# A Fourier and Hyena encoder layer on one core: the filter network's two hidden layers with the positions' halves stacked on the partitions

## The chip, the cores and the metric

The kernel runs on one core of a Trainium2 chip. The metric is the device time of one execution in microseconds, as the median of several runs. Its engines are TensorE (PE in the profile, PEld for its weight loads), VectorE (DVE), ScalarE (ACT), GpSimd (POOL) and SyncE (SP, which issues most DMAs).

## The reference

The layer is applied to two inputs of 1024 positions by 1024 channels. Each goes through an RMS norm and one projection; a Fourier branch takes a two-dimensional DFT (over positions and over 256 channels of each of four groups) of one part; a Hyena branch runs two long convolutions whose filters come from a small network over the positions; both are gated, projected, merged and added to the input. The change touches the filter network, which does not depend on the inputs:

```python
pos = jnp.arange(L, dtype=f32)                       # L = 1024
t = pos / (L - 1)
bands = jnp.linspace(1e-4, FILT_BANDS - 1, FILT_BANDS, dtype=f32)
ang = (2.0 * math.pi * pos / L)[:, None] * bands[None]
z = jnp.concatenate([t[:, None], jnp.cos(ang), -jnp.sin(ang)], axis=-1)   # 1024 x 33
h = jnp.sin(f1 * (z @ w1 + b1))                      # 1024 x 64
h = jnp.sin(f2 * (h @ w2 + b2))                      # 1024 x 64
h = (h @ w3).reshape(L, N_DIR, H_ORDER, H_WIDTH)
h = h * jnp.exp(-t[:, None, None, None] * jnp.abs(decay)[None])
h = h / jnp.sum(jnp.abs(h), axis=(0, 1), keepdims=True)
# ... the two directions form one kernel of length 2L per channel, and its rfft
```

## The kernel before, in words

Nearly all matmuls take operands split into a rounded part and a remainder (`split`: ScalarE rounds, `sub` on VectorE or GpSimd makes the remainder) and run as three products (`mm3`, L193).

The program has a Fourier phase (to about 220 us), a main phase that begins with the filter stage (16 rounds, one for each order and channel tile, to about 480 us; projections are put between as filling work) and goes on with the convolutions, then gates and outputs.

**Fourier phase.** For the first input, `norm` loads eight row tiles `x`, squares each on ScalarE (`sq`, L319), and after each four of them computes `rs` on VectorE (`rstd`, L241 to L252) and four diagonal tiles `dg` (L324). `xtile` transposes and scales with matmuls against `dg` (`tpx`), writes `xg` on ScalarE (L343), stores it (`d_x`), and forms sums and differences `eo` and their split `eh`, `el`. `weights` loads one block of the projection's weights (`wfv`, two buffers, SP queue), forms `wer`, `wor` and splits them (`we`, `wo`). The projection matmuls `pfv` take both. Behind the first input's norm the table `seq` (2 MB) is loaded on GpSimd's queue. There are four Fourier halves, in the order (input 0, half 0), (0, 1), (1, 1), (1, 0); `fourier_half` runs pfv, the alternating column's `pfx` with its cast `x5t`, the sequence stage (`pse`, `pso`, `sev`, `sst`) and the channel stage (`pP`, `pQ`). The last forms `fA` and `fB` on VectorE, one buffer each, which GpSimd's queue stores to `d_fz`.

**Hidden layers.** `hidden(0, ...)` is called ahead of the first norm, `hidden(1, ...)` behind the third Fourier half. Each runs a plain f32 matmul `phd` (L296) for each half of the 1024 positions and `sin_of` (L258 to L270): seven VectorE steps of argument reduction on 128x512 and one sine on ScalarE. The weights stand twice side by side (33x128, 64x128), so that all 128 output partitions hold the 64 channels twice; the result `hd` is 128x1024 and goes to DRAM (`d_h1`, `d_h`). Layer 2 loads 64 of its rows.

**Rounding of hid.** `phase_main` loads `d_h` into `hidr`, rounds all of it to `hid` on ScalarE (L884) and puts the remainder in partitions 64 to 127, so one matmul with doubled weights `w3s` takes both (`pft`). In program order this stands behind the whole Fourier phase.

**Order.** The order within each engine is not the program's: a planner with its own cost model re-orders the instructions under their dependencies and buffers (`schedule_with_timeline_sim=True`). `tc.issue_after(i)` tells it to place what follows behind instruction `i`.

Of the kernel before, what the change touches and what calls it, by code (L numbers as in the profile page):

```python
# [9 lines left out]
F32 = mybir.dt.float32  # L10
F32R = mybir.dt.float32r
I32 = mybir.dt.int32
AF = mybir.ActivationFunctionType
# [3 lines left out]
P = 128  # L17
D = 1024
L = 1024
# [27 lines left out]
def _tables():  # L47
    t = {}
    s = np.arange(P) + 0.5
    fwd, in0, inv = [], [], []  # L50
    th = np.zeros((P, 8, 6))
    for pi, (f1, hf) in enumerate(PAIRS):
        f = f1 + 8 * (np.arange(P) + P * hf)
        w = 2 * np.pi * f / 2048
        c, sn = np.cos(np.outer(s, w)), np.sin(np.outer(s, w))
        wt = np.full(P, 1 / 1024.0)
        if f1 == 0:
            sn[:, 0] = np.sin(np.pi * s)
# [36 lines left out]
    t["c_alt"] = ae.astype(np.float32).reshape(P, 2 * 86)  # L95
    c = np.arange(P)
    cg = np.cos(2 * np.pi * np.outer(c, c) / 256) / 512
    sg = np.sin(2 * np.pi * np.outer(c, c) / 256) / 512
    sg[0] = 0.0
    sg[:, 0] = 0.0  # L100
    d0 = np.zeros((P, P))
    d0[:, 0] = (1.0 - 2.0 * (c % 2)) / 512
    t["c_chan"] = _hl(np.concatenate([cg, sg, d0], axis=1))
    xs = np.zeros((P, 2, 2, P))
    for g in range(2):
        for r in (g, 32 + g):
# [12 lines left out]
    for m in range(4):  # L119
        order.append(256 * m + 128 + np.arange(P))  # L120
        order.append(256 * m + 127 - np.arange(P))
    order = np.concatenate(order)
    t["c_z"] = np.ascontiguousarray(z[order].T)
    v = np.zeros((P, 14), f32)
    v[:, 0:8] = -tn[order].reshape(8, P).T
    v[:, 8] = 1.0
    v[127, 8] = 0.0
    v[127, 9] = 1.0
    v[1:, 10] = -1.0
    v[1:, 11] = 1.0  # L130
    v[:, 12] = -1.0
    v[0, 12] = 1.0
    t["c_vec"] = v
    t["c_id"] = np.eye(P, dtype=f32)
    return t
# [25 lines left out]
class K:  # L161
# [11 lines left out]
        self.left = self.sub(eng, l, src, h)  # L173

    def stt(self, eng, out, a, s, b, op0=MUL, op1=ADD):
        self.nc.vector.scalar_tensor_tensor(out, a, s, b, op0=op0, op1=op1)  # L176

    def tt(self, eng, out, a, b, op):
        e = self.nc.gpsimd if eng == "pool" else self.nc.vector
# [16 lines left out]
    def setup(self, ctx):  # L196
        tc, nc, a = self.tc, self.nc, self.a
# [18 lines left out]

        def dt(name, shape, dtype=F32):
            return dr.tile(shape, dtype, name=name)
        self.d_h = dt("d_h", [P, L])
        self.d_h1 = dt("d_h1", [P, L])  # L220
        self.d_x = [[dt(f"d_x{b}_{k}", [P, L]) for k in range(8)] for b in range(NB)]
        self.d_fz = [[dt(f"d_fz{b}_{k}", [P, L]) for k in range(8)] for b in range(NB)]
        self.d_k = [[dt(f"d_k{n}_{c}", [P, 32 * P]) for c in range(8)] for n in range(2)]
# [47 lines left out]

    def hidden(self, layer, px, pf):

        nc, a = self.nc, self.a
        h = px.tile([P, L], F32, tag="eo", name=f"hd_{layer}", bufs=2)
        out = [h[:, 0:512], h[:, 512:1024]]
        z = px.tile([P, L], F32, tag="x", name="hd_z", bufs=3)
        if layer == 0:
            w = pf.tile([P, P], F32, tag="sst", name="hd_w", bufs=1)
            self.hfb = px.tile([P, 4], F32, name="hd_fb", bufs=1)  # L280
            nc.sync.dma_start(z[0:33], a["c_z"])
            nc.scalar.dma_start(w[0:33], a["filt_w1"])
            nc.scalar.dma_start(self.hfb, a["filt_fb"])
            w, z = w[0:33], z[0:33]
            y, k = [[pf.tile([P, 512], F32, tag=f"{t}p{n}", name=f"s{t}", bufs=1 + (t == "p")) for n in range(2)]
                    for t in "qp"]
        else:
            nc.sync.dma_start(z[64:128], self.d_h1[64:128])
            w = px.tile([P, P], F32, tag="xg", name="hd_w", bufs=2)
            nc.sync.dma_start(w[64:128], a["filt_w2"])  # L290
            w, z = w[64:128], z[64:128]
            y, k = [px.tile([P, L], F32, tag="x", name="s" + t, bufs=3) for t in "yk"]
            y, k = [[t[:, 0:512], t[:, 512:1024]] for t in (y, k)]
        for n in range(2):
            p = self.psum("mm", 4, "phd")
            nc.tensor.matmul(p, w, z[:, 512 * n:512 * n + 512], start=True, stop=True)  # L296
            self.sin_of(y[n], k[n], out[n], p, self.hfb[:, 2 * layer:2 * layer + 1],
                        self.hfb[:, 2 * layer + 1:2 * layer + 2])
        nc.sync.dma_start(self.d_h if layer else self.d_h1, h)


# [80 lines left out]
    def fourier_half(self, b, half, W, fo, px, pf, begun={}):  # L382

        nc = self.nc
# [58 lines left out]
        vec = self.vec  # L443
# [6 lines left out]
        for g in range(2):  # L450
# [3 lines left out]
            A = pf.tile([P, 1026], F32, tag="fA", name="fA", bufs=1)  # L454
            B = pf.tile([P, 1026], F32, tag="fB", name="fB", bufs=1)
            gg = 2 * half + g
            for n in range(2):
                w = (258, 256)[n]
                ns = slice(258 * n, 258 * n + w)
                pr, qr = (Pp[0][:, ns], Pp[1][:, ns]), (Qp[0][:, ns], Qp[1][:, ns])  # L460
                pP = self.psum("X", 2, "pP")[:, :w]
                self.mm3(pP, (ch[:, 0, 0:P], ch[:, 1, 0:P]), pr, True, False)
                self.mm(pP, cx[:, 0, g, :], PX[:, ns], False, True)
                pQ = self.psum("X", 2, "pQ")[:, :w]
# [4 lines left out]
                Ps = pf.tile([P, 258], F32, tag="fPs", name="fPs", bufs=2)  # L469
                Pm = pf.tile([P, 258], F32, tag="fPm", name="fPm", bufs=1)  # L470
                nc.scalar.copy(Ps[:, :w], pP)
                nc.scalar.activation(Pm[:, :w], pP, AF.Copy, scale=vec[:, 11:12])
                t0 = 258 * n
                w = (258, 255)[n]
                r = slice(0, w)
                self.stt("dve", A[:, t0:t0 + w], pQ[:, r], vec[:, 10:11], Ps[:, r])
                self.add("dve", B[:, t0:t0 + w], pQ[:, r], Pm[:, r])
                w = (258, 254)[n]
                r = slice(0, w)
                self.stt("dve", A[:, 1024 - t0:1024 - t0 - w:-1], pQ[:, r], vec[:, 11:12], Ps[:, r])  # L480
                self.stt("dve", B[:, 1024 - t0:1024 - t0 - w:-1], pQ[:, r], vec[:, 12:13], Pm[:, r])
            nc.gpsimd.dma_start(self.d_fz[b][2 * gg], A[:, 0:1024])
            nc.gpsimd.dma_start(self.d_fz[b][2 * gg + 1], B[:, 0:1024])

    def phase_fourier(self):
        tc, nc, a = self.tc, self.nc, self.a
# [386 lines left out]
    def phase_main(self, nct=8, nb=NB, nf=16):  # L873
        tc, nc, a = self.tc, self.nc, self.a
        with ExitStack() as es:
# [7 lines left out]
            nc.sync.dma_start(hid, self.d_h)  # L883
            nc.scalar.copy(self.hid, hid)  # L884
            self.sub("dve", self.hid[64:128], hid[64:128], self.hid[64:128])
            taps = self.filter_taps(0, 0, self.filter_rates(0, 0, ws), ws)
            self.load_x(0, range(4, 8))
            self.cfw0 = mf.tile([P, 4 * P], F32, name="cfw0")
# [11 lines left out]
            for i in range(nf):  # L900
# [508 lines left out]
def _arrange(inp):  # L1409
    A = np.ascontiguousarray  # L1410
# [65 lines left out]
```

## Time and profile before

| | |
|---|---|
| median of 3 runs | 2426.03 us (2425.84 to 2430.51) |
| profiled execution | 2428.06 us, span 2426.1 us |
| mean granted clock of TensorE | 0.996 |
| TensorE busy | 2379.7 us, 98% |
| VectorE, ScalarE, GpSimd busy | 79%, 44%, 21% |
| instructions | 36569 |

The rows of the profile are read so: a timeline row gives start and length in us, engine, source line, operation, output and inputs by name, shape and count, and in brackets the idle time before it with what ended it. A row of waits gives for a waiting engine and its releaser the total in us, how often, and the longest. A row of a window gives its bounds and length, TensorE's busy time and instruction count, the granted clock (1.00 is full), the DMA engines' busy share and GB/s. A plain f32 matmul such as `phd` leaves several records in the trace.

### The profile page before, as it was taken

The page shows a single profiled execution, that of the slowest core. Times are in us where ns is not written, and L with a number is a line of the kernel's source. Part 1 is how long each engine was busy: PE and PEld are TensorE (multiplying, and loading weights), DVE is VectorE, ACT ScalarE, POOL GpSimd, SP SyncE. Part 2 cuts the span into 40 slices and gives each one's busy share as a digit, 9 for nine tenths or more (in the row PEclk, how much of TensorE's full clock was granted, in tenths as well). Part 3 has the DMA queues.
Part 4 walks back from the last instruction along what each step waited for, and adds up shares of the span by engine and source line. Part 5 has one row for each costly group of instructions (what it writes and reads, how often), then busy time and mean ns, then how long its engine had stood idle before and what let it go on. Part 6 is the DMA issues. An engine that isn't in the chain of part 4 may idle for free.

```text
span 2426.1 us, 36569 instructions
## 1 busy us (share of the span) xinstructions
PE 2379.7 (98%) x13068; PEld 2066.0 (85%) x13068; DVE 1905.1 (79%) x3437; ACT 1070.9 (44%) x2031; POOL 497.9 (21%) x518
## 2 busy tenths in 40 slices
PE   6999999999999999999999999999999999999998
PEld 6988888888888888888888888888888888888886
DVE  7687888888749999999889999866555456665677
ACT  6546577767633333333222222332444444444343
POOL 1331322222133334441000000112100111122111
PEclk9999999999999999999999999999999999999999
DMA  8535655555565555546444444445444667786543
GB/s 278 182 128 200 210 181 170 166 173 171 167 204 178 174 167 186 164 152 210 131 139 140 139 138 140 134 137 175 168 159 158 204 211 253 243 265 212 172 158 131
DMA packets 225967, 428.82 MB, mean 177 GB/s; under 512 B 23590, under 2 KB 87303, under 8 KB 225400
## 3 DMA queue, kind: packets, MB, share of 16 engines
q1 hardware_dynamic: 198588, 333.60, 42.6%
q0 software_dynamic: 27008, 92.86, 11.2%
q8 instruction: 103, 1.69, 0.3%
q14 instruction: 80, 0.66, 0.1%
q10 hardware_dynamic: 188, 0.02, 0.0%
HBM read 290.07 MB, written 136.31 MB: 176 GB/s over the span
## 4 chain that ended last, share of the span: by engine, by line
PE 48%; DMA 2%; DVE 1%; issue 1%; ACT 0%; POOL 0%; SPq 0%; DVEq 0%; ACTq 0%; POOLq 0%
PE pin L193 14%; PE pyh L193 7%; PE pg L193 7%; PE po L193 6%; PE pyf L193 6%; PE pT L193 4%; PE pX L193 4%; DMA wr<-in_w_fo 1%; DMA xraw<-d_x 1%; PE tph L791 1%; DVE xsum L180 0%; DMA wr<-in_w_in 0%; DMA wraw<-in_w_in 0%; DVE wl L180 0%; DVE xsum L176 0%
## 5 line engine op out<-in xcount | busy, mean ns | idle before, releaser
L193 PE MATMUL pin<-xl,wh 128*128 128x512 f32 x1472 | 576.1, 392 | 1.7 <-DVE xl L180 1.6
L193 PE MATMUL pin<-xh,wl 128*128 128x512 f32 x1472 | 577.1, 392 | 0.2
L193 PE MATMUL pin<-xh,wh 128*128 128x512 f32 x1472 | 575.8, 391 | 0.2 <-DMA wh<-d_w 0.2
L180 POOL TENSOR_TENSOR wl<-wr,wh 128x512 fp32r<-128x512 f32 x136 | 254.1, 1869 | 1133.7 <-ACT wh L170 1100.4
L193 PEld LDWEIGHTS pin<-xl,wh 128*128 128x128 f32 x1472 | 277.1, 188 | 55.0 <-DVE xl L180 3.0
L193 PEld LDWEIGHTS pin<-xh,wh 128*128 128x128 f32 x1472 | 277.0, 188 | 53.1 <-DMA wh<-d_w 0.7
L193 PEld LDWEIGHTS pin<-xh,wl 128*128 128x128 f32 x1472 | 277.2, 188 | 52.0 <-POOL wl L180 1.3
L170 ACT CAST wh<-wr 128x512 fp32r<-128x512 f32 x264 | 163.3, 619 | 325.0 <-PE pin L193 96.3
L180 DVE TENSOR_TENSOR wl<-wr,wh 128x512 fp32r<-128x512 f32 x128 | 87.8, 687 | 96.7 <-ACT wh L170 96.7
L193 PE MATMUL pX<-bh,cfwd 128*128 128x256 f32 x768 | 163.1, 291 | 0.2 <-DVE t L180 0.2
L180 DVE TENSOR_TENSOR t<-pX,k 128x1024 f32<-128x1024 f32 x128 | 155.4, 1214 | 6.5 <-PE pX L193 2.5
L193 PE MATMUL pyf<-sf,wh 128*128 128x512 f32 x512 | 157.6, 389 | 0.0
L193 PE MATMUL pyh<-sh,wh 128*128 128x512 f32 x512 | 157.3, 389 | 0.0
L193 PE MATMUL pT<-cinv,yh 128*128 128x256 f32 x768 | 145.6, 284 | 0.0
L170 ACT CAST bh<-b 128x512 fp32r<-128x512 f32 x144 | 88.8, 620 | 107.4 <-DVE b L180 71.8
L193 PEld LDWEIGHTS pX<-bh,cfwd 128*128 128x128 f32 x768 | 127.5, 192 | 2.8 <-DVE t L180 0.6
L193 PEld LDWEIGHTS pT<-cinv,yh 128*128 128x128 f32 x768 | 123.1, 190 | 6.6
L170 ACT CAST yh<-y 128x512 fp32r<-128x512 f32 x96 | 59.5, 619 | 144.7 <-DVE y L180 136.9
L193 PEld LDWEIGHTS pyf<-sf,wh 128*128 128x128 f32 x512 | 96.1, 188 | 19.9
L193 PEld LDWEIGHTS pyh<-sh,wh 128*128 128x128 f32 x512 | 96.1, 188 | 19.9
L193 PE MATMUL pX<-bl,cfwd 128*128 128x256 f32 x384 | 109.3, 285 | 0.6 <-DVE bl L180 0.6
L180 DVE TENSOR_TENSOR bl<-b,bh 128x512 fp32r<-128x512 f32 x144 | 104.2, 727 | 7.0 <-ACT bh L170 6.7
(357 smaller groups left out, 5310.4 us busy)
## 6 DMA issues: line engine op xcount, KB each, us to landing
k<-d_k SPq DMA_DIRECT2D x128, 512.0 KB, 4.1
wr<-in_w_in SPq DMA_DIRECT2D x136, 256.0 KB, 3.3
d_g<-gt SPq DMA_DIRECT2D x124, 256.0 KB, 2.8
d_k<-kt SPq DMA_DIRECT2D x128, 128.0 KB, 2.1
d_k<-kt SPq DMA_DIRECT2D x64, 256.0 KB, 2.3
wr<-in_w_fo POOLq DMA_DIRECT2D x64, 256.0 KB, 4.0
g<-d_g SPq DMA_DIRECT2D x64, 256.0 KB, 4.2
wr<-in_w_ho POOLq DMA_DIRECT2D x64, 256.0 KB, 4.1
```

Of the source, the lines that this page charges most:

```text
L170: self.rounded = nc.scalar.copy(h, src)
L180: return e.tensor_tensor(out, a, b, op=op)
L193: return self.nc.tensor.matmul(out, lhsT, rhs, start=start, stop=stop, skip_group_check=shared)
L791: nc.tensor.transpose(tp[:, q * P:(q + 1) * P], eo[:, e, q], self.ident)
```

## The change

The table `c_z` holds the two halves of the positions on top of each other (66x512 rather than 33x1024), and the weights stand block-wise, the first copy feeding output partitions 0 to 63 from the first half's rows, the second 64 to 127 from the second's. A hidden layer is then one matmul and one sine chain over 128x512, and `d_h1`, `d_h` are 128x512. `hidr` needs all positions on both partition halves, so its load becomes two DMAs. In `fourier_half` the last ScalarE and VectorE instruction of the third half are kept (`self.third`), and the rounding of `hid` is put behind them with `issue_after`.

```diff
-    t["c_z"] = np.ascontiguousarray(z[order].T)
+    t["c_z"] = np.concatenate([z[order[0:512]].T, z[order[512:]].T])
...
-        self.d_h = dt("d_h", [P, L])
-        self.d_h1 = dt("d_h1", [P, L])
+        self.d_h = dt("d_h", [P, 512])
+        self.d_h1 = dt("d_h1", [P, 512])
...
-        h = px.tile([P, L], F32, tag="eo", name=f"hd_{layer}", bufs=2)
-        out = [h[:, 0:512], h[:, 512:1024]]
-        z = px.tile([P, L], F32, tag="x", name="hd_z", bufs=3)
+        h = px.tile([P, 512], F32, tag="eo", name=f"hd_{layer}", bufs=2)
+        z = px.tile([P, L], F32, tag="x", name="hd_z", bufs=3)[:, 0:512]
...
-        for n in range(2):
-            p = self.psum("mm", 4, "phd")
-            nc.tensor.matmul(p, w, z[:, 512 * n:512 * n + 512], start=True, stop=True)
-            self.sin_of(y[n], k[n], out[n], p, self.hfb[:, 2 * layer:2 * layer + 1],
-                        self.hfb[:, 2 * layer + 1:2 * layer + 2])
+        p = self.psum("mm", 4, "phd")
+        nc.tensor.matmul(p, w, z, start=True, stop=True)
+        self.sin_of(y, k, h, p, self.hfb[:, 2 * layer:2 * layer + 1], self.hfb[:, 2 * layer + 1:2 * layer + 2])
         nc.sync.dma_start(self.d_h if layer else self.d_h1, h)
...
-                nc.scalar.activation(Pm[:, :w], pP, AF.Copy, scale=vec[:, 11:12])
+                scaled = nc.scalar.activation(Pm[:, :w], pP, AF.Copy, scale=vec[:, 11:12])
...
-                self.stt("dve", B[:, 1024 - t0:1024 - t0 - w:-1], pQ[:, r], vec[:, 12:13], Pm[:, r])
+                summed = self.stt("dve", B[:, 1024 - t0:1024 - t0 - w:-1], pQ[:, r], vec[:, 12:13], Pm[:, r])
...
+        if (b, half) == (1, 1):
+            self.third = summed, scaled
...
-            nc.sync.dma_start(hid, self.d_h)
-            nc.scalar.copy(self.hid, hid)
-            self.sub("dve", self.hid[64:128], hid[64:128], self.hid[64:128])
+            for i in range(2):
+                nc.sync.dma_start(hid[64 * i:64 * i + 64].rearrange("p (n t) -> p n t", n=2),
+                                  self.d_h.rearrange("(n p) t -> p n t", n=2))
+            with tc.issue_after(self.third[0].ins), tc.issue_after(self.third[1].ins):
+                nc.scalar.copy(self.hid, hid)
+                self.sub("dve", self.hid[64:128], hid[64:128], self.hid[64:128])
...
-    o["filt_w1"] = A(np.concatenate([inp["filt_w1"][0]] * 2, axis=1))
-    o["filt_w2"] = A(np.concatenate([inp["filt_w2"][0]] * 2, axis=1))
+    twice = lambda w: np.concatenate([np.pad(w, ((0, 0), (0, 64))), np.pad(w, ((0, 0), (64, 0)))])
+    o["filt_w1"] = A(twice(inp["filt_w1"][0]))
+    o["filt_w2"] = A(twice(inp["filt_w2"][0]))
```

More of the change, by code (lines that the diff above doesn't have):

```diff
@@ L175, in stt @@
     def stt(self, eng, out, a, s, b, op0=MUL, op1=ADD):
-        self.nc.vector.scalar_tensor_tensor(out, a, s, b, op0=op0, op1=op1)
+        return self.nc.vector.scalar_tensor_tensor(out, a, s, b, op0=op0, op1=op1)
     def tt(self, eng, out, a, b, op):
@@ L274, in hidden @@
         nc, a = self.nc, self.a
-        h = px.tile([P, L], F32, tag="eo", name=f"hd_{layer}", bufs=2)
-        out = [h[:, 0:512], h[:, 512:1024]]
-        z = px.tile([P, L], F32, tag="x", name="hd_z", bufs=3)
+        h = px.tile([P, 512], F32, tag="eo", name=f"hd_{layer}", bufs=2)
+        z = px.tile([P, L], F32, tag="x", name="hd_z", bufs=3)[:, 0:512]
         if layer == 0:
-            w = pf.tile([P, P], F32, tag="sst", name="hd_w", bufs=1)
+            w = pf.tile([P, P], F32, tag="sst", name="hd_w", bufs=1)[0:66]
             self.hfb = px.tile([P, 4], F32, name="hd_fb", bufs=1)
-            nc.sync.dma_start(z[0:33], a["c_z"])
-            nc.scalar.dma_start(w[0:33], a["filt_w1"])
+            z = z[0:66]
+            nc.sync.dma_start(z, a["c_z"])
+            nc.scalar.dma_start(w, a["filt_w1"])
             nc.scalar.dma_start(self.hfb, a["filt_fb"])
-            w, z = w[0:33], z[0:33]
-            y, k = [[pf.tile([P, 512], F32, tag=f"{t}p{n}", name=f"s{t}", bufs=1 + (t == "p")) for n in range(2)]
-                    for t in "qp"]
+            y, k = [pf.tile([P, 512], F32, tag=f"{t}p0", name=f"s{t}", bufs=1 + (t == "p")) for t in "qp"]
         else:
-            nc.sync.dma_start(z[64:128], self.d_h1[64:128])
+            nc.sync.dma_start(z, self.d_h1)
             w = px.tile([P, P], F32, tag="xg", name="hd_w", bufs=2)
[L290 to L293, printed above, removed]
-        for n in range(2):
-            p = self.psum("mm", 4, "phd")
-            nc.tensor.matmul(p, w, z[:, 512 * n:512 * n + 512], start=True, stop=True)
-            self.sin_of(y[n], k[n], out[n], p, self.hfb[:, 2 * layer:2 * layer + 1],
-                        self.hfb[:, 2 * layer + 1:2 * layer + 2])
+            nc.sync.dma_start(w, a["filt_w2"])
+            t = px.tile([P, L], F32, tag="x", name="syk", bufs=3)
+            y, k = t[:, 0:512], t[:, 512:1024]
+        p = self.psum("mm", 4, "phd")
+        nc.tensor.matmul(p, w, z, start=True, stop=True)
+        self.sin_of(y, k, h, p, self.hfb[:, 2 * layer:2 * layer + 1], self.hfb[:, 2 * layer + 1:2 * layer + 2])
         nc.sync.dma_start(self.d_h if layer else self.d_h1, h)
```

## The prediction

> **What bounds the kernel now.** I read the page first, then the waits of TensorE, then the windows, then the two stretches that the change touches.
>
> ```profile
> PE 2379.7 (98%) x13068; PEld 2066.0 (85%) x13068; DVE 1905.1 (79%) x3437; ACT 1070.9 (44%) x2031; POOL 497.9 (21%) x518
> ```
>
> TensorE is busy for 2379.7 of 2426.1 us. All its idle time together is 46.4 us, and no change that leaves its matmuls alone can win more than that and what a slow clock costs. VectorE and ScalarE have room on average, so fewer VectorE instructions are worth something only where TensorE stands still for one of them. The waits of TensorE name those places (waited for: us in total, times, longest):
>
> ```profile
> PE tpx L193 <- DVE dg L324: 14.0, 2, 8.8
> PE tpx L193 <- ACT xg L343: 3.1, 2, 2.1
> PE pQ L193 <- DVE fB L176: 2.0, 1, 2.0
> PE pfv L193 <- DVE we L180: 1.7, 2, 0.9
> PE pse L193 <- DVE x5t L180: 1.2, 2, 0.7
> PE pin L193 <- DVE xl L180: 1.6, 2, 1.0
> ```
>
> The first two lie in the first 40 us, where hidden layer 1 of the filter network shares VectorE and ScalarE with the norm; the next two lie between 165 and 215 us, where layer 2 and the rounding of `hid` stand among the third Fourier half. The windows show the clock there (us, PE busy and count, PEclk, DMA share, GB/s):
>
> ```profile
> 300.00:360.00 60.00, 59.85 (x345) 1.00 0.56 177
> 33.30:36.70 3.40, 1.54 (x13) 1.00 1.03 406
> 36.80:40.10 3.30, 3.12 (x14) 0.50 0.73 267
> 204.00:207.40 3.40, 1.39 (x12) 1.00 0.86 281
> 207.50:210.80 3.30, 3.30 (x18) 0.50 0.63 247
> ```
>
> After the layers, in the filter stage, TensorE is full (59.85 of 60.00). And each of the two idle stretches, at 33.3 and 204.0, is followed by about 3.3 us at clock 0.50: a further 3.3 x 0.5 = 1.65 us lost each.
>
> **Layer 2, at 167 us.** Two matmuls become one, and two chains of eight instructions one.
>
> ```profile
> 167.36 1.98 PE L296 MATMUL phd<-hd_z,hd_w 64*128 64x512 f32 x4
> 169.27 0.51 PE L193 MATMUL pfv<-we,eh 128*128 128x260 f32 x2
> L261 DVE TENSOR_SCALAR sk<-sk 128x512 f32<-128x512 f32 x2 | 1.7, 883 | 0.0
> L269 DVE TENSOR_SCALAR sy<-sy 128x512 f32<-128x512 f32 x2 | 0.7, 408 | 0.0
> ```
>
> The pair holds TensorE for 169.27 - 167.36 = 1.91 us; the new one has twice the rows but the same 512 columns, so half goes: -0.95. VectorE loses seven instructions of 0.41 to 0.88 us, 2.9 to 6.2 us. They stood ahead of the `we` remainders that pfv waits for, twice for 1.7 us; the longer wait, 0.9, falls in this stretch and goes: together **-1.9**. The rest of the chain lies beside pfv matmuls, as before.
>
> **The start.** Here one matmul and one chain go too, but TensorE is waiting for `dg` anyway, and the order changes. VectorE now has the `wer`, `wor`, `we`, `wo` of weight blocks 2 and 3 ahead of the second `dg` (six instructions more), and those of blocks 4 and 5 ahead of the first `eo`; before, blocks 4 and 5 came behind it.
>
> ```profile
> 23.17 0.88 DVE L324 TENSOR_SCALAR dg<-ident,rs 128x128 f32<-128x128 f32 x4
> 23.97 0.42 DVE L180 TENSOR_TENSOR wer<-wfv 128x260 f32<-128x260 f32 x1
> 24.31 0.42 DVE L180 TENSOR_TENSOR wor<-wfv 128x256 f32<-128x256 f32 x1
> 27.81 1.29 DVE L180 TENSOR_TENSOR eo<-xg 128x512 f32<-128x512 f32 x2 [1.06 <-ACT xg L343]
> 30.23 1.22 PE L193 MATMUL pfv<-we,eh 128*128 128x260 f32 x8 [0.29 <-ACT eh L170]
> 201.82 0.40 PE L193 MATMUL pfv<-wo,eh 128*128 128x256 f32 x2
> 202.06 0.28 PE L193 MATMUL pfv<-wo,el 128*128 128x256 f32 x1
> 36.98 1.44 PE L193 MATMUL tpx<-dg,x 128*128 128x128 f32 x5 [2.14 <-ACT xg L343]
> 17.89 8.03 SPq L363 DMA_DIRECT2D wfv<-in_w_fv  x4
> DMA to landing us min/median/max: 2.8/3.3/8.2
> DMA to landing us min/median/max: 8.2/8.8/9.5
> seq<-in_c_seq POOLq DMA_DIRECT2D x1, 2064.0 KB, 8.4
> ```
>
> Six instructions at 24.31 - 23.97 = 0.34 put the second `dg` 2.0 us later, less about 1 us that the missing sine and chain give: some +1. That does not bind: the first `eo` now waits for the load of block 5. The two landing rows are those of the `wfv` loads issued from 17.8 to 25.0 and from 24.7 to 25.6: with the `seq` load of 2064 KB not yet in flight they took 2.8 and 3.3 us, beside it 8.2 and 9.5. Block 5's load is issued when `wor` of block 3 has freed its buffer, two places ahead of the second `dg` now, 24.2 - 2 x 0.34 = 23.5 (25.4 before); `seq` is issued behind the same norm's `rs`, just after. It lands between 23.5 + 2.8 = 26.3 and 23.5 + 9.5 = 33.0; I take 28.3 (4.8 us), nearer to the loads that were ahead of `seq`. From the landing, eight short instructions (8 x 0.34, 2.5 with the casts beside them) lead to `eo`; `eo` to the first pfv took 30.23 - 27.81 = 2.4; the 36 matmuls of two such groups, at (202.06 - 201.82) / 2 = 0.12, are 4.3; some 0.7 for the casts of `xg` between. TensorE is back at its next transposes 9.9 us after the landing, at 38.2, where it was at 36.98: +1.2, with ends -0.8 and +5.9. The half clock behind 36.98 may go with its gap, or move to the gap that now opens before pfv; I take half of 1.65 off: the start costs **+0.5**. The Trainium skill, "TensorE: Matmul & The Clock Gate", Part 1, has the clock halved after an idle window of about 3.4 us and tells to avoid idle gaps over that. The rows have 2.14 and 2.01 us of wait before a half clock, so shorter gaps do it here; by the page's length nothing would be taken off and the start would cost +1.2.
>
> **The end of the third half, 200 to 214 us.** In the order of the changed kernel the ten matmuls of pQ and pP 10 and 11 move into the last pfv group, and pQ 11 stands some 14 matmuls further back, so the stores of `fA` and `fB` have landed when it is due: the 2.01 us wait goes, and 1.65 of half clock with it. With layer 2's 1.9, TensorE could be 5.5 us early at the pfx matmuls. It cannot keep it, because of ScalarE's queue:
>
> ```profile
> L883 SPq DMA_DIRECT2D hidr<-d_h x1: 327/327/327, 202.2 to 202.2; - x1
> DMA to landing us min/median/max: 4.7/4.7/4.7
> 207.42 1.03 ACT L884 CAST hid<-hidr 128x1024 fp32r<-128x1024 f32 x1
> 208.36 0.40 ACT L170 CAST w3s<-w 128x256 fp32r<-128x256 f32 x1
> 208.67 0.42 ACT L621 ACTIVATE dec<-dec 128x256 f32<-128x256 f32 x1
> 209.10 1.28 ACT L641 ACT_TABLE_LOAD   x1
> 212.01 0.35 ACT L407 CAST x5t<-pfx 36x260 fp32r<-36x260 f32 x1
> 213.30 0.38 ACT L430 COPY sev<-pse 128x258 f32<-128x258 f32 x1 [0.93 <-PE pse L193]
> 207.01 0.70 PE L193 MATMUL pQ<-qp,chan 128*128 128x256 f32 x3 [2.01 <-DVE fB L176]
> 212.88 0.51 PE L193 MATMUL pse<-alt,x5t 128*128 128x258 f32 x2 [0.72 <-DVE x5t L180]
> ```
>
> The `hidr` load is still released by a late matmul of the last pfv group, ten places further on: 202.2 - 1.9 + 10 x 0.12 = 201.5. It is now two loads, one behind the other; with 4.7 to land, and up to 1.3 for the second, 206.2 to 207.5, taken as 206.9. The new order on ScalarE is `hid`, `w3s`, `x5t`, `dec`, table load, four `ex`, `sev`. Start to start that is 0.94 + 0.31 + 0.35 + 0.43 + 2.91, so `sev` starts at 206.9 + 4.9 = 211.8, against 213.30. TensorE is ready before that, first held by `x5t` (0.72 before, now 2 to 3 us), then by `sev` for about 1 us. So of 5.5 us this stretch keeps **-1.5**. The `issue_after` on `hid` only fixes a place that its rounding already had: 0. Behind it, the pin matmuls' wait for `xl` (1.6 in all) shrinks, since the `xl` loads stand behind pfx, which is earlier: **-0.5**, between 0 and -1.6.
>
> **The filter stage.** Its instructions are permuted too, and TensorE has nothing to win there: 0, and only upward. Sum: +0.5 - 1.5 - 0.5 = -1.5. The profiled execution took 2428.06 us, its span 2426.1 and 1.96 around it, 2.03 above the median of the runs, so it becomes about 2426.6; on the median the forecast is 2426.03 - 1.5 = **2424.5**. A measurement of this kernel can tell about 0.2%, 4.85 us, from no change: below 2421.2 is faster, above 2430.9 slower.
>
> **Rivals.**
> *Both gaps gone and nothing in their place.* Block 5 lands at 26.3, the half clock at 36.8 does not come (-0.8 - 1.65), and `hidr` is early enough that ScalarE is through with `hid` before pfx ends (-5.5). That is 2426.0 - 8.0 = 2418, and 2420 with half of the second. For it: each wait named is one that VectorE sets. Against it: the ScalarE row sum above.
>
> *The weights' load in the shadow of `seq`.* The place is the start: block 5 takes 8.2 to 9.5 us as its neighbours did, lands at 31.7 to 33.0, and the start costs +4.6 to +5.9 instead of +0.5. The total is 2428.6 to 2429.9, slower than before. It decides from a landing of about 5.6 us on, where the start's cost eats the 2.0 behind it. For it: `seq` is issued within 1 us of that load. Against it: the load is ahead.
>
> *The permuted filter stage stalls in order.*
>
> ```profile
> L180 DVE TENSOR_TENSOR bl<-b,bh 128x512 fp32r<-128x512 f32 x144 | 104.2, 727 | 7.0 <-ACT bh L170 6.7
> wr<-in_w_in SPq DMA_DIRECT2D x136, 256.0 KB, 3.3
> ```
>
> One remainder of 727 ns put ahead of one that TensorE needs costs up to 0.73 in each of 16 rounds, 11.6 us: 2436 at full size, over 2430.9 from nine rounds on. For it: VectorE's queue is in order. Against it: the window from 300 to 360 shows 0.15 us of idle TensorE in 60.
>
> *The two loads of `hidr` go one after the other.* Each moves 256 KB, and such loads land in 3.3 us: 6.6 instead of 4.7, `sev` at 213.0, and the total at 2425.7. The Trainium skill, "DMA: Bandwidth & Descriptors", Rules for kernel authors, says of two transfers to disjoint partition halves that they serialize, and asks for one of 128 partitions; no run here shows a pair yet.
>
> *The change does not reach TensorE.* Layer 2's work was hidden, every gap stays: 2426.
>
> **How the numbers follow.** The forecast 0.48, with its own range 2422 to 2428; both gaps gone 0.18; `seq`'s shadow 0.15; the filter stage 0.08; the loads in series 0.06; nothing 0.05. Faster by over 0.2% is nearly all of the second and a little of the first's tail: 0.20. Slower by over 0.2% is the filter stage and the upper end of `seq`'s shadow: 0.15. The rest, 0.65, is within. Range 2419.5 to 2430.0: it leaves out half of the first rival and most of the filter stage's.
>
> **What would show it.** One phd matmul of about 0.9 us per layer and no wait of pfv for `we` behind it; the first `eo` directly behind the remainders of blocks 4 and 5, its start 2.5 us behind their landing; no wait of pQ for `fB` at the third half, but pse waiting 2 to 3 us for `x5t` and then for `sev`; `sev` near 212. The forecast is wrong if TensorE comes to the filter stage more than 3 us earlier or later than before, or if waits of over 0.3 us come up between 240 and 480 us.

## The result, and the profile after

The changed kernel takes 2429.32 us (median of 22 runs, 2427.19 to 2433.0) where the kernel before took 2427.3 (22 runs, 2423.51 to 2430.51). The ratio is 1.0013, 95% interval 1.0007 to 1.0019: between 1.7 and 4.6 us slower, 3.2 by the ratio (the two medians alone lie 2.0 apart). The forecast was 1.5 us faster. The time lies in the predicted range and the difference within 0.2%, but it has the other sign.

The page of the changed kernel (busy us, share of the span, instructions) shows the removed work: TensorE 2.8 us and VectorE 9.3 us less.

```profile
PE 2376.9 (98%) x13064; PEld 2066.2 (85%) x13064; DVE 1895.8 (78%) x3423; ACT 1070.0 (44%) x2029; POOL 501.2 (21%) x518
```

Its span is 2426.9 us (profiled execution 2428.66), 0.8 us more than that of before with less work: idle time took it back. The waits of TensorE (total us, times, longest) say where:

```profile
PE tpx L193 <- DVE dg L320: 15.9, 2, 8.5
PE tpx L193 <- ACT xg L339: 3.2, 2, 2.1
PE pse L193 <- DVE x5t L180: 3.0, 2, 2.5
...
PE pse L193 <- ACT sev L426: 1.9, 1, 1.9
PE pft L193 <- ACT sev L426: 1.3, 1, 1.3
...
PE pfv L193 <- ACT eh L170: 1.1, 1, 1.1
PE pin L193 <- POOL wl L180: 0.8, 1, 0.8
```

The two waits of before that the prediction counted on (pQ for `fB` 2.0, pfv for `we` 1.7 in all) have shrunk to 0.3 and 0.6. In their place stand `x5t` (1.2 before, now 3.0), `sev`, and `eh` (0.3 before); the wait for `dg` in the start has grown from 14.0 to 15.9. The windows of the third half's end (bounds, length, busy time and count of TensorE, its weight loads, VectorE, ScalarE and GpSimd, then granted clock, DMA share, GB/s):

```profile
209.00:212.00 3.00, 0.92 (x7) 0.70 (x6) 1.68 (x3) 1.63 (x4) 0.76 (x2) 1.00 0.16 39
212.00:215.00 3.00, 1.39 (x8) 1.09 (x8) 0.62 (x3) 2.97 (x6) 0.00 (x0) 0.72 0.98 389
215.00:218.00 3.00, 2.27 (x11) 1.89 (x12) 1.31 (x4) 2.10 (x6) 0.00 (x0) 0.50 1.01 412
218.00:221.00 3.00, 3.00 (x18) 2.86 (x17) 2.90 (x6) 2.34 (x5) 0.00 (x0) 0.64 1.03 422
```

TensorE stands for 4.4 of the 9 us from 209 to 218, and the half clock lasts from the window at 212 into that at 218: (0.28 x 3 + 0.50 x 3 + 0.36 x 3) / 0.50 = 6.8 us at half speed, where before had 3.4.

To add up such places across kernels with different orders, I counted for each trace when TensorE had done a given amount of matmul work, each matmul taken at its full-clock pace. A kernel's **lag** is how many us later than a base it has done what the base had done at some time. The base is the profile of e5 below, which has the order of before on every engine and a shorter profiled execution (span 2421.9). The lags are worked out from all matmul rows but those of phd, and from 225 us on they are read where both kernels have done exactly the same matmuls, so that the pace assumed for one doesn't enter. The nine kernels whose start has the old order lie between 0 and 1.8 at 60 us, so a single us means little.

| us | 60 | 165 | 200 | 212 | 225 | 480 |
|---|---|---|---|---|---|---|
| before | 0.3 | 0.9 | 1.0 | 1.0 | 1.0 | 0.8 |
| after | 2.9 | 3.3 | 2.0 | 0.6 | 5.0 | 5.3 |

Against before, the change loses 2.4 us up to 165, gains 2.8 from there to 212, loses 4.4 from 212 to 225, and 0.5 up to 480. The profile of before fell 4.2 us behind that of e5 in all, 3.5 of them after 1100 us, where the change does nothing; that is why the two spans differ by 0.8 only.

**The start.** The rows of TensorE, ScalarE and VectorE, then SP's stores of `xg`, and the landing time of the `wfv` loads issued between 24.5 and 27 us:

```profile
38.09 4.45 PE L193 MATMUL tpx<-dg,x 128*128 128x128 f32 x24 [2.09 <-ACT xg L339]
60.74 1.24 PE L193 MATMUL pfv<-we,eh 128*128 128x260 f32 x8 [1.10 <-ACT eh L170]
36.43 0.41 ACT L170 CAST we<-wer 128x260 fp32r<-128x260 f32 x1 [0.18 <-DVE wer L180]
37.35 1.26 ACT L339 ACTIVATE xg<-tpx,gpre 128x512 f32<-128x512 f32 x2 [0.51 <-DMA d_x<-xg]
28.63 1.30 DVE L180 TENSOR_TENSOR eo<-xg 128x512 f32<-128x512 f32 x2 [0.23 <-ACT xg L339]
28.56 2.00 SPq L340 DMA_DIRECT2D d_x<-xg  x2
DMA to landing us min/median/max: 8.7/8.7/8.7
```

And of before, the same store and the same `xg`:

```profile
27.73 1.36 SPq L344 DMA_DIRECT2D d_x<-xg  x2
36.24 1.27 ACT L343 ACTIVATE xg<-tpx,gpre 128x512 f32<-128x512 f32 x2
```

`eo` starts at 28.63: block 5 had landed by some 26.1, the predicted 2.5 us earlier, so near the early end of its bounds. By the prediction's formula TensorE would be back at 26.1 + 9.9 = 36.0, and just there it runs out of work; but it is back at 38.09 only, with a gap of 2.09 for `xg`. ScalarE has casts of a weight block ahead of that `xg` (its load took 8.7 us, its remainder came at 35.05), but they are done at 36.84. What ends the wait last is the store of an earlier `xg` to `d_x`, which frees the buffer: issued at 28.56, it took 8.3 us beside `seq`, and `xg` starts at 37.35. In before the store was issued at 27.73 and took 8.4 us, and `xg` started at 36.24. The store is issued when ScalarE has written both halves of the first `xg`, and in the new order casts of early weight blocks stand ahead of the first half (26.65) and between the two (27.55). And at 60.74 there is a wait for `eh` that before did not have.

**Layer 2.**

```profile
169.66 1.02 PE L293 MATMUL phd<-hd_z,hd_w 128*128 128x512 f32 x2
170.12 0.81 PE L193 MATMUL pfv<-we,eh 128*128 128x260 f32 x2
```

The step over phd is 170.12 - 169.66 = 0.46 us, where it was 1.91. The two pfv matmuls behind it take longer, 0.64 us to the next row at 170.76 where before had 0.34, so 1.15 is won. Of the wait of pfv for VectorE's `we`, 0.9 in this stretch before, 0.4 is left, and 0.2 for ScalarE's `we` is new. The lag shows 1.4 won in all from 165 to 200 us.

**The end of the third half.** ScalarE, then SP's queue, the landing of `hidr`, and the first matmul of the filter stage:

```profile
209.18 1.05 ACT L885 CAST hid<-hidr 128x1024 fp32r<-128x1024 f32 x1 [2.48 <-DMA hidr<-d_h]
210.44 0.36 ACT L403 CAST x5t<-pfx 36x260 fp32r<-36x260 f32 x1
211.99 0.42 ACT L619 ACTIVATE dec<-dec 128x256 f32<-128x256 f32 x1 [1.20 <-DMA dec<-in_filt_decay]
215.33 0.35 ACT L426 COPY sev<-pse 128x258 f32<-128x258 f32 x1
204.38 1.34 SPq L882 DMA_DIRECT2D hidr<-d_h  x2
207.05 0.58 SPq L617 DMA_DIRECT2D dec<-in_filt_decay  x1
208.62 5.63 SPq L719 DMA_DIRECT2D xl<-d_x  x8
DMA to landing us min/median/max: 3.6/3.6/3.6
219.83 0.56 PE L193 MATMUL pin<-xh,wh 128*128 128x512 f32 x1
```

And of before, the first load of `xl` and its first pin matmuls:

```profile
L721 SPq DMA_DIRECT2D xl<-d_x x1: 431/431/431, 205.7 to 205.7; - x1
L193 PE MATMUL pin<-xh,wh x3: 392/397/404, 215.5 to 219.6; 128*128 128x512 f32 x3
```

`sev` comes at 215.33, not 211.8: `hid` starts 2.3 us later than I had it (209.18 for 206.9), and 1.2 come behind it. `hidr` was issued 2.9 us later than I had it; and ScalarE, through with `x5t` at 210.80, waits 1.2 us for `dec`, whose load stands on SP behind `hidr` and both loads of `w`, 2.7 us behind the first of `hidr`. The loads of `xl` stand behind that, 2.9 us later than before.

### The profile page after: what moved, and what is told of

Same layout as the page of the kernel before. It is cut to its first block, busy times and chain, and to the rows that moved or that the text cites. A ratio compares the mean times of both kernels' runs of the same rounds, so it can differ in the third digit from the quotient of the medians.

```text
span 2426.9 us, 36543 instructions
## 1 busy us (share of the span) xinstructions
PE 2376.9 (98%) x13064; PEld 2066.2 (85%) x13064; DVE 1895.8 (78%) x3423; ACT 1070.0 (44%) x2029; POOL 501.2 (21%) x518
## 4 chain that ended last, share of the span: by engine, by line
PE 49%; DMA 2%; issue 2%; DVE 1%; ACT 0%; POOL 0%; DVEq 0%; ACTq 0%; POOLq 0%
PE pin L193 16%; PE pg L193 7%; PE po L193 6%; PE pyf L193 6%; PE pyh L193 6%; PE pT L193 4%; PE pX L193 4%; DMA wr<-in_w_fo 1%; PE tph L789 1%; DMA wr<-in_w_ho 0%; DMA wh<-d_w 0%; POOL wr L1151 0%; DVE wl L180 0%; ACT wh L170 0%; DVE o L176 0%
## 5 line engine op out<-in xcount | busy, mean ns | idle before, releaser
L193 PE MATMUL pT<-cinv,yl 128*128 128x256 f32 x384 | 109.5, 285 | 0.1
```

Source lines behind the costliest of these rows:

```text
L193: return self.nc.tensor.matmul(out, lhsT, rhs, start=start, stop=stop, skip_group_check=shared)
```

## The experiments

Each time is a median; the kernel before had 2425.26 us on the chip of e1 to e4, 2426.03 on that of e5 to e8, 2426.16 and 2426.35 beside e9 and e10, and e11. The verdicts go by the ratio with its interval, from which the quotient of two medians can be 0.0005 away.

**e1: layer 1 alone.** Layer 1 as in the change, the rest as before.

```diff
-        self.d_h1 = dt("d_h1", [P, L])
+        self.d_h1 = dt("d_h1", [P, 512])
...
+        nc.sync.dma_start(z[64:128].rearrange("p (n t) -> p n t", n=2), self.d_h1.rearrange("(n p) t -> p n t", n=2))
```

> Only layer 1 in the new form; layer 2, its stores and the load of hidr as before. On every engine the order is the changed kernel's up to about 150 us and the kernel before's from there. Theory: the start loses 1.2 us at its transposes and 2.6 us by the first pse, as in the changed kernel's trace, and nothing gives it back, so 2.6 us over the kernel before, ratio 1.001. Rival (the start only looks late, and the loss comes from the end of the third half alone): within 0.5 us of the kernel before.

2429.12 us, ratio 1.0014 (1.0005 to 1.0023), some 3.4 us slower.

```profile
PE pQ L193 <- ACT qp L170: 2.0, 1, 2.0
```

A loss as large as that of the whole change is there with layer 1 alone. The wait of 1.10 us for `eh` comes at 60.23, as in after. TensorE has a lag of 2.3 us at 60, and 4.9 at 165 after a wait of pQ for `qp` of 2.0, behind which it runs at half clock from 98.3 to 101.7 us. e5 lacks that wait, but before has it with 1.3 and after with 1.2, so it is not the new order's alone.

**e2: layer 2 alone.** Layer 1 as before, layer 2 as in the change.

```diff
+            for n in range(2):
+            nc.sync.dma_start(z[64 * n:64 * n + 64], self.d_h1[64 * n:64 * n + 64, 512 * n:512 * n + 512])
```

> Only layer 2 in the new form; layer 1 as before. The order is the kernel before's up to about 150 us and the changed kernel's from there. Theory (the queue of ScalarE at hid): 1.7 us won at layer 2, 2.5 at pQ, then 4.5 lost in the waits for x5t and sev with their half clocks on top (6.3 in the trace) and about 1 to 2 in the filter stage: at 300 us between 2.5 and 4 us later than before, and the whole 1 to 3 us slower. Rival (the loss is the start's, layer 2 is a gain as forecast): 1 to 2 us faster than before.

2425.45 us, ratio 1.0002 (0.9993 to 1.0011): level. Its lag goes from 2.0 at 165 to -0.7 at 212, and then to 3.2 at 225, as in after. So the gain of layer 2 is real, and the end of the third half takes it back and more in this profile; by the runs the two come out level.

**e3: `hid` rounded one place later.** The change, but the rounding stands behind `x5t` of the last half.

```diff
-        if (b, half) == (1, 1):
-            self.third = summed, scaled
+        halved = nc.scalar.copy(X5[0:36], p5)
+        cast = self.sub("dve", X5[32:36], p5[32:36], X5[32:36])
+        if (b, half) == (1, 0):
+            self.third = cast, halved
```

> The changed kernel with hid's rounding put behind the cast of x5t in the last Fourier half. Theory: pse's wait for x5t shrinks from 2.5 us to about 1 (w3s still stands ahead of x5t), the first sev comes ahead of the table load, so its wait of 1.9 us goes; 2 to 4 us come back by 225 us with the half clocks, and the kernel is 1 to 3 us faster than the changed one. Rival (the waits are set by the landing of the loads, wherever hid stands): no change against the changed kernel, within 0.5 us.

2426.65 us, ratio 1.0006 (0.9998 to 1.0015). The waits from 165 to 240 us are now 1.6 for `x5t`, 0.5 for `sev` and a new 1.0 of pin for `xh`. Its lag at 225 is 2.6, against 5.0, but 1.2 of this difference were there at 165, where the two kernels have the same order. From 200 to 225 it loses 1.9 where after loses 3.0: some of the loss may hang on ScalarE's order. The interval is too wide to say that it is faster than the change.

**e4: everything on ScalarE out of the way.** Layer 1 as before, layer 2 new, `hid` behind `x5t`, and `dec`, `w3s`, the table load and the first four `ex` behind `sev`.

```diff
+            if (b, half, tag, len(out), e) == (1, 0, "T", 1, 0):
+                self.staged = added, evened
...
+            rates = self.filter_rates(0, 0, ws, self.staged[1])
+            with tc.issue_after(self.staged[0].ins), tc.issue_after(self.staged[1].ins):
+                taps = self.filter_taps(0, 0, rates, ws)
```

> Layer 1 as before, layer 2 in the new form, hid's rounding behind x5t and dec, w3s, the table load and the four ex behind the 34-row sev. Theory: no wait of pse for x5t over 0.7 us and none for sev over 0.5 until the ex; TensorE reaches the filter stage 2 to 4 us ahead of the kernel before, and the whole is 2 to 4 us faster than before (ratio 0.998 to 0.999). Rival (what is won there is given back when pft waits for its operands, or in the re-ordered filter stage): no faster than before.

2431.64 us, ratio 1.0025 (1.0015 to 1.0036): 6 us slower, the worst. The waits for `x5t` and `sev` are gone, and TensorE is 4.3 us ahead of e5 at 212. Then:

```profile
214.20 1.04 ACT L170 CAST xh<-xl 128x1024 fp32r<-128x1024 f32 x1 [2.83 <-DMA xl<-d_x]
215.30 0.80 PE L193 MATMUL pin<-xh,wh 128*128 128x512 f32 x1 [3.27 <-ACT xh L170]
```

ScalarE waits for the load of `xl`, TensorE for ScalarE, and at 225 the lag is 5.2: 9.5 us lost in 13, with 3.4 us at half clock in it. Taking ScalarE's work out of the way is not enough; the landing of `xl` lies right behind it. (A further 2.7 us go by 480, with pin waiting 2.8 for `wl`.)

**e5: `issue_after` alone.** The kernel before with only the rounding of `hid` fixed behind the third half.

```diff
-            nc.scalar.copy(self.hid, hid)
-            self.sub("dve", self.hid[64:128], hid[64:128], self.hid[64:128])
+            with tc.issue_after(self.third[0].ins), tc.issue_after(self.third[1].ins):
+                nc.scalar.copy(self.hid, hid)
+                self.sub("dve", self.hid[64:128], hid[64:128], self.hid[64:128])
```

> The kernel before with only the issue_after on hid's rounding. The order on each of the five engines is the same as the kernel before's, so it is a second look at that kernel. Theory: ratio 1.000, and between 800 and 2200 us, where every profile so far came out 3.4 to 5 us ahead of the one profile of the kernel before, this one does too (that profile was a long execution of its kernel). Rival (the later stages do gain by the change): this profile follows the first one there, within 1 us.

2424.57 us, ratio 0.9997 (0.9988 to 1.0006). In the traces the order of all five engines is the same as without, so in the kernel before that part of the change does nothing. No run has the changed kernel without it.

**e6: the start in the old order.** The change, with weight blocks 2 and 3 behind the second `dg` and blocks 4 to 7 each behind the `el` of the block four earlier.

```diff
+                        with tc.issue_after(self.dged.ins) if k in (2, 3) else tc.issue_after(els[k - 4].ins) if k > 3 else ExitStack():
+                            self.weights(pw, W, 0, k, True)
```

> The changed kernel with the weight blocks of the start held back: blocks 2 and 3 behind the second dg, blocks 4 to 7 behind el of the block four earlier. Theory (the start's loss is the order of the weight blocks, not layer 1 itself): the transposes come back at 36 to 37 us rather than 38.1, no wait of pfv for eh of 1.1 us near 60, the first pse at 60 to 61.5 us, and the whole 1.5 to 3 us faster than the changed kernel, level with the kernel before. Rival (layer 1's new form itself costs it, or the loads in the shadow of seq do in either order): the same as the changed kernel within 0.5 us.

2426.3 us, ratio 1.0004 (0.9995 to 1.0013).

```profile
36.59 2.31 PE L193 MATMUL tpx<-dg,x 128*128 128x128 f32 x12 [1.78 <-ACT xg L339]
```

TensorE is back at 36.59 rather than 38.09, no wait comes up between 40 and 62 us, and the lag is 0.3 at 60 and 1.2 at 165. The store of `xg` is issued at 27.31 here; in e6, before and after TensorE is back 9.3, 9.3 and 9.5 us behind that issue. Over all kernels, the three with the new order of the start (after, e1, e3) have a mean lag of 3.4 at 165 (2.1 to 4.9), the nine others (e7 has an order of its own) 1.1 (0 to 2.1). The new layer 1 itself costs nothing that the profile shows; the place that the planner gave the weight blocks does. This rests on the traces: by the intervals of the runs, e6 and the change (1.0007 to 1.0019) can't be told apart.

**e7: `seq` out of the way of the weights.** The change, with the loads of `seq` and `chan` released by weight block 7 instead of the norm.

```diff
-                            nc.gpsimd.tensor_copy(fo[t][:, 0, 0:1], self.rs[:, 7:8])
+                            nc.gpsimd.tensor_copy(fo[t][:, 0, 0:1], W[1][0][:, 7, 0:1])
```

> The changed kernel with the loads of seq and chan released by weight block 7 instead of the norm's rs, so no wfv load has them beside it. Theory (the loads in the shadow of seq hold the start): all wfv loads land in 2.6 to 4 us instead of 8.7 for the two late ones, TensorE goes on with the transposes at 32 to 35 us rather than 38.1, and seq lands near 48, 12 us before it is needed: 2 to 4 us faster than the changed kernel. Rival (ScalarE and VectorE set the pace of the start anyway): gain under 1 us, as the transposes' wait moves to eh and el.

2429.68 us, ratio 1.0013 (1.0004 to 1.0022): as slow as the change.

```profile
34.53 1.95 PE L193 MATMUL tpx<-dg,x 128*128 128x128 f32 x16
PE pfv L193 <- ACT eh L170: 2.3, 3, 1.1
DMA to landing us min/median/max: 2.7/2.7/2.7
```

The `wfv` loads that took 8.7 us now take 2.7, and TensorE is back at its transposes 3.6 us earlier, at 34.53. But between 36 and 165 us pfv waits 2.3 us for `eh`, and the lag at 165 is 4.6. The shadow of `seq` is there (the stores of `xg` take 3.7 us without it, 8.3 with it), and taking it away wins nothing: the pace of ScalarE and VectorE in the new order is next.

**e8: e4 without its last step.** Layer 1 as before, layer 2 new, `hid` behind `x5t`. The lines against e4:

```diff
-            rates = self.filter_rates(0, 0, ws, self.staged[1])
-            with tc.issue_after(self.staged[0].ins), tc.issue_after(self.staged[1].ins):
-                taps = self.filter_taps(0, 0, rates, ws)
+            taps = self.filter_taps(0, 0, self.filter_rates(0, 0, ws), ws)
```

> Layer 1 as before, layer 2 in the new form, hid's rounding behind x5t. Theory: e3 without the start's loss: 1.5 to 3 us faster than e3, and 0 to 2 us faster than the kernel before; at 213 us 3 to 4 us ahead, of which the xl loads at 420 GB/s (they all start when pfx ends, 4.2 MB, 10 us) take back most by 225 us. Rival (the win at 213 us stays): 3 us and more ahead at 240 us.

2424.87 us, ratio 1.0000 (0.9991 to 1.0009). Windows of the same stretch (after's are above):

```profile
209.00:212.00 3.00, 1.51 (x13) 1.30 (x13) 1.02 (x4) 2.21 (x4) 0.00 (x0) 1.00 0.97 383
212.00:215.00 3.00, 1.20 (x8) 0.78 (x6) 0.69 (x1) 3.00 (x7) 0.00 (x0) 1.00 1.03 416
215.00:218.00 3.00, 2.63 (x16) 2.11 (x16) 2.83 (x6) 2.02 (x4) 0.00 (x0) 1.00 1.03 421
```

TensorE is idle for 3.7 us from 209 to 218, nearly as long as in after, yet the clock stays full throughout. e3 has the same order in this stretch and 6.8 us at half speed. The same window of both, 203 to 228, first e3, then e8:

```profile
203.00:228.00 25.00, 21.14 (x118) 17.93 (x117) 18.26 (x35) 17.29 (x30) 2.51 (x4) 0.86 0.71 261
203.00:228.00 25.00, 18.61 (x111) 14.83 (x111) 18.22 (x34) 18.00 (x30) 3.48 (x5) 1.00 0.72 266
```

Idle time plus half of the slow time is 3.9 + 3.4 = 7.3 us in e3 and 6.4 + 0 in e8: without the slow clock TensorE runs into the next waits instead (`sev` 3.1, pin for `xl` 1.5). By the lag, which compares equal work, e3 loses 1.9 us from 203 to 228 and e8 2.4. In this pair the slow clock took its time from waits that were there anyway. What goes with its coming is in the last section, as far as the traces show it.

**e9: `hid` finished in the third half.** Layer 1 as before. Layer 2 rounds and splits its sine at once and stores the finished `hid`; the main phase loads it, and its cast and remainder are gone.

```diff
+        self.split(hh, hl, h, "dve", "act")
...
-                nc.scalar.copy(self.hid, hid)
-                self.sub("dve", self.hid[64:128], hid[64:128], self.hid[64:128])
+            nc.sync.dma_start(self.hid.bitcast(F32), self.d_h)
```

> Layer 1 as before, layer 2 in the new form, and hid rounded and split right behind its sine, in the third Fourier half, where ScalarE and VectorE have room; it goes to DRAM finished, and the main phase loads it straight into its place: the cast of 1.03 us and the subtraction of 1.22 us leave the stretch at 205 to 215 us. ScalarE's order there is w3s, dec, x5t, table load, four ex, sev. Theory (ScalarE's queue with the late loads of w3 and dec holds TensorE, hid or not): x5t still waits for dec's landing near 210, pse waits 2 to 3 us for x5t and 1 to 2 us for sev, and the whole is level with e2, within 1 us. Rival (hid's cast and subtraction are what holds x5t): x5t's wait under 1 us and 2 us faster than e2.

2425.91 us, ratio 1.0001 (0.9992 to 1.0009).

```profile
210.53 0.42 ACT L632 ACTIVATE dec<-dec 128x256 f32<-128x256 f32 x1 [1.63 <-DMA dec<-in_filt_decay]
210.85 0.35 ACT L416 CAST x5t<-pfx 36x260 fp32r<-36x260 f32 x1
PE pse L193 <- DVE x5t L180: 2.5, 1, 2.5
```

With the cast of `hid` gone, TensorE waits the same 2.5 us for `x5t`. It is `dec` that waits now, for its landing, and `x5t` is queued behind it. So taking the cast away is not enough. But the planner has also put `dec` ahead of `x5t`, which stood behind it in after, so e9 does not show that the cast cost nothing there.

**e10: e9 and the filter's taps behind `sev`.** The step of e4 on top of e9, here behind the second `sev` of the last half.

```diff
+            if (b, half, tag, len(out), e) == (1, 0, "X", 2, 0):
+                self.staged = added, evened
```

> e9 with dec, w3s, the table load and the four ex put behind the second sev of the last half. Theory (ScalarE's order): no wait of pse for x5t or sev over 0.7 us, 4 us ahead of the kernel before at 212 us, and since ScalarE has 1 us less to do than in e8, at 240 us 1 to 2 us ahead of it and the whole 1 to 3 us faster than before. Rival (the xl loads set when pin can go on): the win at 212 us is gone by 225, as pin waits for xh and xl, and the kernel is level with the kernel before.

2425.62 us, ratio 0.9999 (0.9990 to 1.0008). No wait for `x5t` or `sev` is left, the lag at 212 is -3.4, and at 225 it is +2.8:

```profile
213.18 1.04 ACT L170 CAST xh<-xl 128x1024 fp32r<-128x1024 f32 x1 [2.60 <-DMA xl<-d_x]
```

As in e4 the load of `xl` is next, although it is issued earlier here than in after (205.96 for the first): all eight are issued in one row and none lands early.

**e11: the first `xl` ahead on SP.** e10, with SP's order written out: first `xl`, `hid`, three more `xl`, the filter weights and `dec`, the other four `xl`.

```diff
+            self.load_x(0, range(1))
...
+                last = nc.sync.dma_start(self.hid.bitcast(F32), self.d_h)
+            with tc.issue_after(last.ins):
+                self.load_x(0, range(1, 4))
```

> e10 with SP's queue turned round behind the last pfv: the load of the first xl, then hid, then xl 1 to 3, then w3, dec and db, and xl 4 to 7. ScalarE's order follows: x5t, two sev, the first xh, and dec, w3s, the table load and the four ex only behind the fourth xh. Theory (the landing of the xl loads, the first of them above all, is what pin waits for): the first xl is issued near 203 instead of 206, pin starts 2 to 3 us earlier than in e10, no slow-clock stretch follows it, and at 225 us it stands 0 to 2 us ahead of the kernel before instead of 3.5 behind; the whole 1 to 3 us faster than before. Rival (the eight transfers of 4.2 MB as a whole hold it): pin starts earlier, but the same 3 us are waited out by 230 us, and the kernel stays level with the kernel before.

2425.72 us, ratio 0.9995 (0.9986 to 1.0004).

```profile
192.85 0.42 SPq L734 DMA_DIRECT2D xl<-d_x  x1
209.91 1.05 ACT L170 CAST xh<-xl 128x1024 fp32r<-128x1024 f32 x1
211.27 0.40 PE L193 MATMUL pin<-xh,wh 128*128 128x512 f32 x1
```

The first `xl` goes out at 192.85 already, not near 203 as expected. The first pin matmul starts at 211.27 without a wait, pin's waits for `xh` fall from 3.0 to 0.2 us (those for `xl` rise from 0.8 to 2.1), and the lag at 225 is -0.5 instead of 2.8. So what SP has in its queue, and in what order it lands, holds much of the end of the third half. How much is not separated: with SP's order the planner also changed those of ScalarE and TensorE, and e10 has 6.8 us of half clock in this stretch, e11 none. The whole is not clear of level: by 600 us about 2 us of it are given back, with pin waiting 1.9 for `wl` from GpSimd. It has the lowest ratio of the kernels, and is not shown to beat the kernel before.

## Why the prediction was wrong, point by point

The sum was +0.5 for the start, -1.9 for layer 2 counted into -1.5 for the third half's end, and -0.5 behind it. By the lag it is +2.4, -2.8, +4.4 and +0.5 in the four stretches, +4.5 by these two profiles up to 480 us; by the ratio of all runs it is 3.2 (1.7 to 4.6). (The start's own terms, 1.2 less half of 1.65, give +0.4 rather than +0.5.) Of the prediction's own signs of being wrong two came: TensorE comes to the filter stage 4.0 us later than before, and between 240 and 480 us pin waits 0.8 for `wl`.

**The start: the place was right, the step and the size were not.** By their lags, e1 and e6 show that the loss comes with layer 1 and goes with the old order of the weight blocks. The step that failed is the end of the chain from the landing of block 5. The landing was early, and up to 36.0 us the chain held; but where it has 0.7 for the casts of `xg`, TensorE waits 2.09, because the buffer of `xg` comes free only when the store to `d_x` has landed, 8.3 us after its issue, and the new order issues it 0.8 us later. Even without the slow landings (e7) the order costs as much further on, so the number was not in any one landing. The half clock that I took half off came all the same. What share is the waits at 38 and 60 us, and what the later wait of pQ for `qp`, was not separated.

**Layer 2: right in mechanism, a little too large.** 1.15 us of matmul work and 0.3 of waits, against 0.95 and 0.9 forecast: 1.4 by the lag for 1.9. e2 shows the same (1.3) with layer 1 left alone.

**The third half's end: the step that failed most.** That the pQ wait would go (0.3 left) and that TensorE would be stopped by `x5t` for 2 to 3 us (2.5) and then by `sev` (1.9) came out. The size did not, in three terms. `hidr` was issued at 204.38, not 201.5: 2.4 of these 2.9 us are the start's loss, which this sum left out altogether, its own +0.5 too, and 0.5 is what layer 2 gave less. The sum for ScalarE was one of busy times, with nothing for the landing of `dec`, which now ends later than `x5t`: 1.2 us here, and 1.6 in e9 without the cast. And the gaps brought 6.8 us of half clock, where I had the 3.3 go away. The window from 203 to 228 us, first of before, then of after:

```profile
203.00:228.00 25.00, 21.34 (x129) 18.04 (x128) 19.41 (x37) 17.80 (x30) 3.15 (x5) 0.93 0.82 296
203.00:228.00 25.00, 19.03 (x120) 16.38 (x119) 16.41 (x34) 16.01 (x30) 1.06 (x2) 0.86 0.72 262
```

TensorE is idle 25.00 - 19.03 = 6.0 us against 3.7, and the clock costs (0.93 - 0.86) x 25 = 1.75 more. TensorE was idle for 1.9 us of after's half clock, so half of these, 0.95, are counted twice: 3.1 together, which is what after's lag rises by from 200 to 225 (3.0).

**Behind it: wrong in sign.** I had the wait for `xl` shrink because pfx is earlier. Of its 1.6 us only 0.6 lie here, the rest behind 480 us; they did go, but because TensorE came later, and waits of pft for `sev` (1.3) and of pin for `wl` (0.8) are new. The `xl` loads stand behind `hidr`, `w` and `dec` on SP, and start 2.9 us later than before (208.62 for 205.7). Eight loads of 512 KB at the 420 GB/s of the windows need 10.0 us. In e4 and e10 this is plainly the next wait, and e11 takes most of it away.

**`issue_after`: right**, 0, as far as e5 shows it in the kernel before.

**The rivals.** *`seq`'s shadow* gave a total that holds the one found, 2428.6 to 2429.9, but by luck: block 5 landed early, and e7 without the shadow is as slow. The shadow was on the stores of `xg` instead, in before as much as in after. *The loads of `hidr` in series* fell: the cast starts 4.8 us behind the first issue, where one load took 4.7, not 6.6. The Trainium skill, "DMA: Bandwidth & Descriptors", Rules for kernel authors, says that halves serialize and that splitting is no use; in these rows the pair neither won nor lost over the single load. *Both gaps gone* fell with `x5t`. *The filter stage* costs 0.5 us by the lag (pin for `wl`, 0.8), far from its 11.6; in e4 it takes 2.7, and in e11 about 2.

Open: how much of after's 4.4 us between 212 and 225 is typical of its 22 runs, and what share of it is `dec`, what the half clock and what the landing of `xl`. The ratio says less than its one profile does.

## What to carry to other kernels

When a stall of the bound engine goes, sum up what comes next including the landings of loads, and of the stores that free a buffer, not the busy times of the queue alone: look at which loads are queued on the issuing engine ahead of the one that is needed first, and write that order out if need be. Under a planner a small edit can cost through the place that unrelated work gets; compare the orders of the two builds, and test by fixing the old order with the edit kept (e6). And take a second profile of the same order as a base before reading differences of a few us: here two such profiles differed by 4.2.

## What the runs showed of the hardware

From 26 to 2390 us of the 13 traces the half clock comes in stretches of 3.41 us, one or two in a row. Within a trace all their bounds lie on one grid of 3.41 us, whose position differs from trace to trace. The busy time of TensorE in the grid window ahead goes with it: all 18 windows at full clock with under 1.6 us of busy time were followed by half clock, 7 of the 15 with 1.6 to 2.0, and none of the 8927 with more. So a gap of 2.0 to 2.5 us brings a half clock if one window holds most of it, and may bring none if two windows share it. Two grid windows of e5, whose order is that of before, and two of e8:

```profile
32.64:36.05 3.41, 3.02 (x24) 2.81 (x24) 2.27 (x5) 0.76 (x3) 0.00 (x0) 1.00 0.96 341
36.05:39.46 3.41, 1.81 (x16) 1.81 (x16) 2.82 (x7) 2.47 (x5) 0.20 (x2) 1.00 0.85 285
207.96:211.37 3.41, 1.83 (x16) 1.52 (x16) 2.04 (x4) 1.59 (x3) 0.00 (x0) 1.00 0.70 270
211.37:214.78 3.41, 1.82 (x14) 1.29 (x12) 0.51 (x1) 3.40 (x8) 0.00 (x0) 1.00 1.02 414
```

The gap of 1.99 us in e5 is shared, and the clock stays full; the same gap in before, 2.14 us, falls into one window with 1.54 us busy, and half clock follows. In e8 two windows share the idle time; a window from 206.8 us would have had 1.22 us busy. In e3 the windows ahead of its two stretches have 1.79 and 1.90, which lies where both happen. No run sets the grid, so this is read from the traces and not tested. The Trainium skill, "TensorE: Matmul & The Clock Gate", Part 1, has the activity judged in free-running windows of 3.4 us; the length and the grid agree. Its bound of about 3.4 us on idle gaps is too long for this case.
